# The low part of every second weight chunk of the second feed-forward stage: from a VectorE subtraction to a negated ScalarE copy and an adding transfer

## The chip, the cores and the metric

The kernel runs on one core of one Trainium2 chip. The metric is the device time of one execution in microseconds. The core has five engines with instruction streams of their own: TensorE (PE) multiplies matrices, VectorE (DVE), ScalarE (ACT) and GpSimd (POOL) work on elements, and SyncE (SP) issues transfers. Transfers run on 16 DMA engines. ScalarE and GpSimd can issue transfers too. In the profile's lines PEld is TensorE's load of its stationary operand.

## The reference

One block of a network on 256 tokens of width 2048, in float32: a gated feed-forward stage (inner width 5632), a mixer of two branches (a state-space scan and a gated spatial unit) whose results are merged, a second gated feed-forward stage, and a last norm.

```python
def swiglu_ffn(h, w_gate, w_up, w_down):
    return (jax.nn.silu(h @ w_gate) * (h @ w_up)) @ w_down
...
        h = rms_norm(x, ffn1_norm[i])
        x = x + 0.5 * swiglu_ffn(h, ffn1_w_gate[i], ffn1_w_up[i], ffn1_w_down[i])
        h = rms_norm(x, mix_norm[i])
        proj = h @ w_in[i]
...
        merged = g_a * (y_a @ w_branch_a[i]) + g_b * (y_b @ w_branch_b[i])
        x = x + merged @ w_out[i]
        h = rms_norm(x, ffn2_norm[i])
        x = x + 0.5 * swiglu_ffn(h, ffn2_w_gate[i], ffn2_w_up[i], ffn2_w_down[i])
    return rms_norm(x, final_norm)
```

The change lies in the line before the last: the weights of the second `swiglu_ffn`.

## The kernel before

All weights are read once, as chunks of 128 x 2048 float32 (1 MB), in one list `chunks` of 356 that is filled by `add` and `add_ffn` (lines 104 to 134) in the order in which they are used. Chunks 0 to 131 are the first feed-forward stage, 132 to 223 the mixer and its output, 224 to 355 the second feed-forward stage. A feed-forward stage has three groups (4, 4 and 3 blocks of 512 inner columns). In a group each block takes four gate chunks and four up chunks, and then the group's down weights follow (16, 16 and 12 chunks).

TensorE multiplies in the type float32r, which keeps fewer bits than float32. To keep the accuracy, each operand is held as two float32r parts: the high part is the value rounded to float32r, and the low part is the rest, value minus high part. A product is then the sum of three: high by high, high by low, and low by high. For a weight chunk `split_to` (line 151) does this: ScalarE copies the raw chunk into `whi` (line 148, which rounds it), and VectorE subtracts `whi` from the raw chunk into `wlo` (line 149).

A chunk has four columns of work for TensorE (`step`, line 212, called by `job`): each takes 512 columns of the chunk and issues six matmuls, for two halves of the tokens the lines 216 (`whi`), 217 (`wlo`) and 218 (`whi`). So a chunk is 24 matmuls of 512 columns.

The order of work is written out by hand (a manual schedule). `take` calls `tick` before each column of work. At the first column of chunk c, `tick` first issues what was left to do for earlier results (hooks that fall due, then the evacuations in `pend`) and then `split_to(c + 2)` (LOOK = 2). That issues the load of chunk c + 4 on SP's queue (`load_to`, line 139) and the split of chunk c + 2. There are three raw buffers, three `whi` and three `wlo` (NRAW and NSPL). So chunk c + 2 takes the `whi` and `wlo` of chunk c - 1, and its split can begin when TensorE has ended that chunk; the load of chunk c + 4 takes the raw buffer of chunk c + 1 and can begin when that one has been split. Each engine works through its instructions in the order in which they were issued.

The evacuations of the feed-forward stages are: after a gate job two Silu passes on ScalarE (line 318), after an up job a multiplication on VectorE (line 328) and, two columns of work later, transposes on TensorE (line 258) with a split of the result on ScalarE and VectorE (lines 244 and 245); after a down job an addition on VectorE (line 293). The start of the last group's down part (`down_out`, line 1014) issues a 1 MB load on POOL's queue, of the final norm's gain into the tile `fin` (line 1017). It is POOL's only work in the second feed-forward stage.

Of the kernel before, what the change touches and what calls it, by code (L numbers as in the profile page):

```python
# [12 lines left out]
AF = mybir.ActivationFunctionType  # L13
ALU = mybir.AluOpType
# [12 lines left out]
SUB = 2048  # L27
# [18 lines left out]
def f(ap):  # L46
    return ap.bitcast(F32)
# [3 lines left out]
def kernel(  # L51
# [31 lines left out]
    act, dve, pe, pool = nc.scalar, nc.vector, nc.tensor, nc.gpsimd  # L83
# [20 lines left out]
    chunks = []  # L104

    def add(w, a=0, n=None):
        chunks.extend(w[i] for i in range(a, w.shape[0] if n is None else a + n))

    def add_ffn(wg, wu, wd, first):
        j, d = 0, 0  # L110
        for n in GROUPS:
            for _ in range(n):
                if j == 0 and first is not None:
                    add(first)
                else:
                    i = j - (first is not None)
                    add(wg, 4 * i, 4)
                    add(wu, 4 * i, 4)
                j += 1
            add(wd, d, 4 * n)  # L120
            d += 4 * n
# [8 lines left out]
    add(w_ga, 12, 4)  # L130
    add(w_ba)
    add(w_out)
    add_ffn(w2g, w2u, w2d, None)
    NSUB = len(chunks)

# [3 lines left out]
    def load_to(i):  # L139
        while st["load"] <= min(i, NSUB - 1):  # L140
            j = st["load"]
            t = wp.tile([P, SUB], F32, tag="raw", name="raw", bufs=NRAW)
            nc.sync.dma_start(out=t, in_=chunks[j])
            raws[j] = t
            st["load"] += 1

    def split_piece(hi, lo, r, s):
        act.activation(out=hi[:, s], in_=r[:, s], func=AF.Copy)  # L148
        dve.tensor_tensor(out=lo[:, s], in0=r[:, s], in1=f(hi[:, s]), op=ALU.subtract)  # L149

    def split_to(i):
        while st["split"] <= min(i, NSUB - 1):
            j = st["split"]
            load_to(j + NRAW - 1)
            r = raws.pop(j)
            hi = wp.tile([P, SUB], F32R, tag="whi", name="whi", bufs=NSPL)
            lo = wp.tile([P, SUB], F32R, tag="wlo", name="wlo", bufs=NSPL)
            split_piece(hi, lo, r, slice(0, SUB))
            splits[j] = (hi, lo)
            st["split"] += 1  # L160

# [12 lines left out]
    def tick():  # L174
        for fn in hooks.pop(st["tick"], ()):
            fn()
        while pend:
            pend.pop(0)()
        if st["off"] == 0:
            split_to(st["sub"] + LOOK)  # L180
            splits.pop(st["sub"] - 1, None)
        credit[0] += credit[1]
        while fillers and credit[0] >= 1.0:
            try:
                next(fillers[0])
                credit[0] -= 1.0
            except StopIteration:
                fillers.pop(0)
        if not fillers:
            credit[0] = 0.0  # L190
        st["tick"] += 1
# [572 lines left out]
    st["split"] = 1  # L764
    split_h1(2)
    split_to(1)
    split_h1(4)
    for i in range(5):
# [379 lines left out]
```

## Time and profile before

| what | us |
|---|---|
| median of 2 runs (2087.6 and 2088.61) | 2088.11 |
| the profiled execution, as timed | 2085.11 |
| the profiled execution's span, first to last instruction | 2083.3 |
| line 149 on VectorE, the low part, 355 whole chunks: each | 2.292 |
| line 148 on ScalarE, the high part, 355 whole chunks: each | 1.915 |
| lines 216 to 218 on TensorE, one matmul as shown | 0.39 |

The span is what the profile's positions and shares refer to; the time as timed is 1.8 us longer. Matmuls are pipelined: one is shown as lasting 0.39 us, but a new one starts about every 0.23 us. A line of the timeline gives start, duration, engine, line of the kernel, operation, output and inputs, and in brackets how long the engine was idle before it and whom it waited for. A line of the waits gives the waiting engine and line, whom it waited for, and the total in us, how often, and the longest. A line of the stages gives the busy time and number of instructions of TensorE, its weight load, VectorE, ScalarE and POOL, then the granted TensorE clock (1.00 is full), the share of time in which the DMA engines were busy, and GB/s. A line of the transfers gives how many, the size of each, and the median time from issue to landing.

### The profile page before, as it was taken

To read this page: it belongs to the slowest core of one execution; us is meant where nothing else is said; L and a number is where in the kernel's file an instruction comes from. 1 tells how busy PE (TensorE), PEld (TensorE's weight loads), DVE (VectorE), ACT (ScalarE), POOL (GpSimd) and SP (SyncE) were. 2 spreads that over 40 slices of the span, in tenths; PEclk is the share of its full clock that TensorE was granted. 3 is DMA by queue.
4 is the path that set the end of the run, shared out by engine and by line. 5 is a ranking of instruction groups with operands and counts; after the bars stand their busy time and mean duration, and the time that the engine had idled before them with its cause. 6 is when DMAs were issued, how large, how long until landed. Compare 5 with 4: busy or idle time off the path is not lost. (4 is left out here: it accounts for less than half of the span.)

```text
span 2083.3 us, 23136 instructions
## 1 busy us (share of the span) xinstructions
PE 2034.3 (98%) x9764; PEld 1681.5 (81%) x9764; DVE 1126.6 (54%) x1095; ACT 862.8 (41%) x702; POOL 73.0 (4%) x135
## 2 busy tenths in 40 slices
PE   8999999999999999999989899999999999999997
PEld 6888888887888888878777788888888888888886
DVE  4765665546664555556555665554454444544454
ACT  5543344443334454443333544443433334333443
POOL 0000001111000000011100000000000000000000
PEclk9999999999999999999999999999999999999999
DMA  7457766555655455566555455555555555555553
GB/s 305 182 197 240 244 222 210 190 201 180 221 204 195 171 191 213 191 236 211 200 200 188 170 182 182 202 198 186 191 193 191 193 184 187 194 199 185 189 180 117
DMA packets 65769, 412.20 MB, mean 198 GB/s; under 512 B 10192, under 2 KB 10592, under 8 KB 19840
## 3 DMA queue, kind: packets, MB, share of 16 engines
q1 hardware_dynamic: 52848, 376.49, 50.6%
q0 software_dynamic: 10800, 30.03, 4.5%
q10 hardware_dynamic: 2016, 4.20, 0.6%
q8 instruction: 76, 1.25, 0.2%
q14 instruction: 29, 0.24, 0.0%
HBM read 398.21 MB, written 12.45 MB: 197 GB/s over the span
## 5 line engine op out<-in xcount | busy, mean ns | idle before, releaser
L149 DVE TENSOR_TENSOR wlo<-raw,whi 128x2048 fp32r<-128x2048 f32 (+1 forms) x359 | 815.8, 2274 | 789.3 <-ACT whi L148 789.2
L148 ACT ACTIVATE whi<-raw 128x2048 fp32r<-128x2048 f32 (+1 forms) x359 | 681.5, 1901 | 907.1 <-PE acc L218 832.0
L216 PE MATMUL acc<-whi,h 128*128 128x512 f32 x1856 | 728.7, 393 | 5.9 <-ACT whi L148 5.9
L217 PE MATMUL acc<-wlo,h 128*128 128x512 f32 x1856 | 724.8, 391 | 4.8 <-DVE wlo L149 4.8
L218 PE MATMUL acc<-whi,h 128*128 128x512 f32 x1856 | 724.2, 390 | 0.0
L216 PEld LDWEIGHTS acc<-whi,h 128*128 128x128 f32 x1856 | 349.7, 188 | 79.5 <-ACT whi L148 7.0
L217 PEld LDWEIGHTS acc<-wlo,h 128*128 128x128 f32 x1856 | 349.7, 188 | 78.0 <-DVE wlo L149 6.7
L218 PEld LDWEIGHTS acc<-whi,h 128*128 128x128 f32 x1856 | 349.6, 188 | 73.2
L216 PE MATMUL acc<-whi,gt 128*128 128x512 f32 x704 | 276.0, 392 | 0.0
L218 PE MATMUL acc<-whi,gt 128*128 128x512 f32 x704 | 276.0, 392 | 0.0
L217 PE MATMUL acc<-wlo,gt 128*128 128x512 f32 x704 | 275.1, 391 | 0.0
L217 PEld LDWEIGHTS acc<-wlo,gt 128*128 128x128 f32 x704 | 132.5, 188 | 28.7
L218 PEld LDWEIGHTS acc<-whi,gt 128*128 128x128 f32 x704 | 132.6, 188 | 28.0
L216 PEld LDWEIGHTS acc<-whi,gt 128*128 128x128 f32 x704 | 132.6, 188 | 27.9
L318 ACT ACTIVATE t<-acc,rc 128x512 f32<-128x512 f32 x44 | 27.9, 686 | 69.4 <-PE acc L218 69.4
L216 PE MATMUL acc<-whi,mT 128*128 128x512 f32 x128 | 50.2, 392 | 0.0
L218 PE MATMUL acc<-whi,mT 128*128 128x512 f32 x128 | 49.8, 389 | 0.0
L217 PE MATMUL acc<-wlo,mT 128*128 128x512 f32 x128 | 49.8, 389 | 0.0
L293 DVE SCALAR_TENSOR_TENSOR x_sb<-acc,x_sb 128x1024 f32<-128x1024 f32 x27 | 33.1, 1225 | 27.6 <-PE acc L218 27.6
L273 ACT ACTIVATE junk<-x_sb 128x512 bf16<-128x512 f32 x32 | 20.2, 631 | 64.6 <-DVE x_sb L293 53.0
L328 DVE SCALAR_TENSOR_TENSOR t<-acc,rc,t 128x512 f32<-128x512 f32 x44 | 31.0, 746 | 21.7 <-PE acc L218 21.6
L244 ACT ACTIVATE gt<-q 128x512 fp32r<-128x512 f32 x44 | 23.9, 596 | 31.3 <-PE q L258 31.3
(195 smaller groups left out, 1031.2 us busy)
## 6 DMA issues: line engine op xcount, KB each, us to landing
raw<-in_w1d_dram SPq DMA_DIRECT2D x44, 1024.0 KB, 4.9
raw<-in_w2g_dram SPq DMA_DIRECT2D x44, 1024.0 KB, 4.8
raw<-in_w2u_dram SPq DMA_DIRECT2D x44, 1024.0 KB, 4.8
raw<-in_w2d_dram SPq DMA_DIRECT2D x44, 1024.0 KB, 4.8
raw<-in_w1g_dram SPq DMA_DIRECT2D x40, 1024.0 KB, 4.9
raw<-in_w1u_dram SPq DMA_DIRECT2D x40, 1024.0 KB, 4.9
raw<-in_w_in_dram SPq DMA_DIRECT2D x24, 1024.0 KB, 4.8
raw<-in_w_gb_dram SPq DMA_DIRECT2D x16, 1024.0 KB, 4.9
```

What stands on the lines that cost most here:

```text
L148: act.activation(out=hi[:, s], in_=r[:, s], func=AF.Copy)
L149: dve.tensor_tensor(out=lo[:, s], in0=r[:, s], in1=f(hi[:, s]), op=ALU.subtract)
L216: pe.matmul(acc[:, h, :], lhsT=lhs[:, k, 0, t], rhs=hi, start=first, stop=False)
L217: pe.matmul(acc[:, h, :], lhsT=lhs[:, k, 0, t], rhs=lo, start=False, stop=False)
L218: pe.matmul(acc[:, h, :], lhsT=lhs[:, k, 1, t], rhs=hi, start=False, stop=last)
L244: act.activation(out=dst[:, :, 0, :], in_=src, func=AF.Copy)
L273: act.activation(out=j, in_=x_sb[:, h, m * N:m * N + N], func=AF.Square, accum_out=ssq[:, h, m:m + 1])
L293: dve.scalar_tensor_tensor(out=xs, in0=acc, scalar=scale, in1=xs, op0=ALU.mult, op1=ALU.add)
L318: act.activation(out=s[:, h, :], in_=acc[:, h, :], func=AF.Silu, scale=rc(h))
L328: dve.scalar_tensor_tensor(out=s[:, h, :], in0=acc[:, h, :], scalar=rc(h), in1=s[:, h, :], op0=ALU.mult, op1=ALU.mult)
```

## The change

`SECOND` is set to the number of chunks before the second feed-forward stage plus 8, which is 232. From there on the chunks with an even number take another way to their low part. ScalarE makes the high part as before. It then makes a second copy of the raw chunk with the factor -1 into `wlo`, which is the negated high part. A transfer issued by GpSimd then reads the same chunk from HBM a second time and adds it to what `wlo` holds. VectorE does nothing for these chunks. The load of the raw chunk on SP's queue, the odd chunks, and all chunks before 232 are as they were.

```diff
     add(w_out)
+    SECOND = len(chunks) + 8
     add_ffn(w2g, w2u, w2d, None)
     NSUB = len(chunks)
...
             lo = wp.tile([P, SUB], F32R, tag="wlo", name="wlo", bufs=NSPL)
-            split_piece(hi, lo, r, slice(0, SUB))
+            if j >= SECOND and j % 2 == 0:
+                act.activation(out=hi, in_=r, func=AF.Copy)
+                act.activation(out=lo, in_=r, func=AF.Copy, scale=-1.0)
+                pool.dma_start(out=lo, in_=chunks[j], accum_op=ALU.add)
+            else:
+                split_piece(hi, lo, r, slice(0, SUB))
             splits[j] = (hi, lo)
             st["split"] += 1
```

## The prediction

> **What bounds the kernel now.** I read first the head of the page (busy time by engine), then the waits, then the timeline of one chunk in the second feed-forward stage, and last the transfers and the granted clock.
>
> ```profile
> span 2083.3 us, 23136 instructions
> PE 2034.3 (98%) x9764; PEld 1681.5 (81%) x9764; DVE 1126.6 (54%) x1095; ACT 862.8 (41%) x702; POOL 73.0 (4%) x135
> PE acc L217 <- DVE wlo L149: 4.8, 4, 1.8
> DVE wlo L149 <- ACT whi L148: 346.2, 131, 4.3
> ACT whi L148 <- PE acc L218: 365.4, 114, 3.6
> 1800.00:2060.00 260.00, 260.00 (x1161) 215.51 (x1160) 126.42 (x72) 101.34 (x73) 0.00 (x0) 1.00 0.51 182
> ```
>
> TensorE is busy for 2034.3 of 2083.3 us. The third line is its longest total of waits for a low part, 4.8 us in the whole run. The next two lines are the waits from 1330 to 2060 us alone, the second feed-forward stage: ScalarE waits for TensorE to free a weight buffer (114 times), VectorE waits for ScalarE; TensorE has no wait at all in that view. The last line is the stage 1800 to 2060 us: TensorE 260.00 of 260.00 us, VectorE 126.42, POOL 0, clock 1.00, the DMA engines 0.51 busy. So this stage is TensorE alone, and VectorE time taken out of it is worth nothing. It can only lose.
>
> How much a low part may be late is read from one chunk:
>
> ```profile
> 1398.26 1.92 ACT L148 ACTIVATE whi<-raw 128x2048 fp32r<-128x2048 f32 x1 [3.52 <-PE acc L218]
> 1403.70 1.92 ACT L148 ACTIVATE whi<-raw 128x2048 fp32r<-128x2048 f32 x1 [3.52 <-PE acc L218]
> 1405.65 2.29 DVE L149 TENSOR_TENSOR wlo<-raw,whi 128x2048 fp32r<-128x2048 f32 x1 [3.15 <-ACT whi L148]
> 1403.50 0.39 PE L216 MATMUL acc<-whi,h 128*128 128x512 f32 x1
> 1403.73 0.39 PE L217 MATMUL acc<-wlo,h 128*128 128x512 f32 x1
> ```
>
> A chunk takes 1403.70 - 1398.26 = 5.44 us. When TensorE has ended chunk c-1, its buffers go to chunk c+2: the ScalarE copy starts at 1403.70, as chunk c starts on TensorE (1403.50; its first low-part matmul is at 1403.73). Chunk c+2's first low-part matmul comes two chunks on, at 1403.73 + 10.88 = 1414.61, so the low part has 10.91 us from the start of the copy. VectorE is done at 1405.65 + 2.29 = 1407.94: 6.7 us to spare.
>
> **The change, part by part.** The chunks are 0 to 355; the second stage begins at 224, so the condition takes the even ones from 232 to 354: 62 chunks, one in each pair of 10.88 us.
>
> *Removed:* 62 subtractions of 2.29 us, 142 us of VectorE. Worth 0: TensorE waits for none of them, and 142 us of VectorE would hide nothing else.
>
> *Second ScalarE pass:* the same shape as the copy, 1.92 us, x62 = 119 us. ScalarE has 101.34 of 260 us busy, so there is room; but the pass stands in the path of the low part, which is there at 1.92 + 1.92 + 0.06 = 3.9 us (0.06 for two hand-overs; from 1403.70 + 1.92 to 1405.65 one took 0.03). It frees the raw buffer then, against 4.24 us before, so SP's loads start no later. Queued behind it on ScalarE are the copies of the next chunk (3.5 us idle before them) and the evacuations in mid-chunk, at most 1.92 us later with their results due chunks later: 0. A gate evacuation in front of the copy takes about 1.2 us off the room of one chunk in eight; that falls into the stall below or the slack beside it: 0, at most 10 x 1.2 = 12 us.
>
> *The adding transfer:* it is issued by POOL once the negated part is there, and may take 10.91 - 3.9 = 7.0 us from issue to landing. Call that time D. No transfer of before adds into its destination; the nearest rows are:
>
> ```profile
> raw<-in_w2g_dram SPq DMA_DIRECT2D x44, 1024.0 KB, 4.8
> x_sb<-in_xk_dram POOLq DMA_DIRECT2D x1, 2048.0 KB, 11.1
> fin<-in_gf_dram POOLq DMA_DIRECT2D x1, 1024.0 KB, 7.5
> ws_sb<-in_wst_dram POOLq DMA_DIRECT2D x1, 512.0 KB, 5.4
> 1342.28 0.60 POOL L1017 DMA_DIRECT2D fin<-in_gf_dram  x1 [198.82 <-PE acc L218]
> ```
>
> A megabyte lands in 4.8 us from SP's queue and in 7.5 us from POOL's, beside the same raw loads. Adding reads two megabytes (weights and the destination) and writes one. Per half megabyte POOL's rows grow by 7.5 - 5.4 = 2.1 us, so a second megabyte read makes 7.5 + 4.2 = 11.7; the row that moves two megabytes says 11.1. Low end: 4.8 (it lands like a raw load; nothing can be gained below, since nobody waits). High end: 2 x 7.5 = 15 (reading the destination and adding do not overlap at all). I take 11.1, the row nearest in bytes read: it is issued by POOL and shares the engines with other loads.
>
> The Trainium skill, page "DMA: Bandwidth & Descriptors", section "Anatomy of one DMA", gives such a POOL transfer 2.0 us plus bytes/436e3: 4.4 us for one megabyte, an estimate of 6.8 us for two. By that rule D is under 7.0 and the change costs nothing; the traced 7.5 and 11.1 stand against it, and the sum goes by the rows.
>
> *From D to time.* A transfer later than 7.0 us makes TensorE wait x = D - 7.0 = 4.1 us. The wait is not paid at every pair. The copy for chunk e+2 starts when chunk e-1 ends, before the wait of e, so e's wait is slack for e+2: the next even chunk is on time, and only the one after waits again. That is 31 waits: 31 x 4.1 = 127 us.
>
> *The clock after a wait.* The trace has such waits in the mixer:
>
> ```profile
> 1061.00 0.39 PE L216 MATMUL acc<-whi,h 128*128 128x512 f32 x1
> 1062.62 0.50 PE L217 MATMUL acc<-wlo,h 128*128 128x512 f32 x1 [1.24 <-DVE wlo L149]
> 1062.96 0.40 PE L218 MATMUL acc<-whi,h 128*128 128x512 f32 x1
> 1063.20 0.39 PE L216 MATMUL acc<-whi,h 128*128 128x512 f32 x1
> ...
> 1107.84 0.50 PE L216 MATMUL acc<-whi,h 128*128 128x512 f32 x1 [0.22 <-ACT whi L148]
> 1110.17 0.64 PE L217 MATMUL acc<-wlo,h 128*128 128x512 f32 x1 [1.82 <-DVE wlo L149]
> 1110.60 0.63 PE L218 MATMUL acc<-whi,h 128*128 128x512 f32 x1
> 1113.59 0.49 PE L216 MATMUL acc<-whi,h 128*128 128x512 f32 x1
> 1113.92 0.39 PE L217 MATMUL acc<-wlo,h 128*128 128x512 f32 x1
> 1114.15 0.40 PE L218 MATMUL acc<-whi,h 128*128 128x512 f32 x1
> ...
> 1110.00:1115.00 5.00, 4.83 (x14) 3.86 (x15) 5.00 (x5) 1.39 (x1) 0.00 (x0) 0.66 0.58 210
> ```
>
> After a wait of 1.24 us the matmuls follow each other by 0.24 us as ever. After one of 1.82 us they follow by 0.43 us, from 1110.17 to 1113.59, and the stage's granted clock is 0.66. Eight steps of 0.43 in place of 0.23 are 1.6 us, with the next (0.33) 1.7 us. A wait of 4.1 us is well past that, so each costs 1.7 us more: 31 x 1.7 = 53 us. (It also lends slack to the next even chunk, which needs none.) The Trainium skill, page "TensorE: Matmul & The Clock Gate", section "Part 1: The HAM clock gate", says that about 3.4 us of idleness halves the clock and about 3.4 us of work restores it; the 3.42 us of slow matmuls agree, while here 1.82 us of waiting were enough. By that rule alone waits of 2 to 3 us would cost no clock; at 4.1 us both give the same sum.
>
> *DMA engines.* One raw load occupies them for 0.51 x 5.44 = 2.77 us. Four chunks need 4 x 2.77 and two adding transfers 2 x 5.54 (two megabytes each): 22.2 us, in a stretch of 21.76 + 4.1 + 1.7 = 27.6 us. They are not the bound, but 0.8 busy. Raw loads have 3 x 5.44 - 4.2 = 12.1 us before they are needed, against 4.8: hidden; without that cover each late microsecond would stop TensorE.
>
> *POOL's queue.* One other issue lies in this stage, the final gain (fin), at 1342.28 before. It is now behind the adding transfers ahead of it in the program, with the third group's down part (chunk 344, which is (344 - 224) x 5.44 = 653 us into the stage), so it leaves some 640 us later. Its first reader starts there after three chunks (16.3 us) and it lands in 7.5: hidden, though one adding transfer shares with it, at most 2.8 us once.
>
> **Sum.** 127 + 53 = 180 us on the profiled execution's span of 2083.3 (2085.11 as timed): 2263 as a span. The runs' median is 2088.11, 3.0 above that execution's time: 2088 + 180 = 2268 us.
>
> **The rivals.** Below, 2% is 42 us, about what a measurement of this kernel can tell from no change.
>
> *Covered, no slower.* The second read is pipelined with the first and the transfer lands like a raw load, D from 4.8 to 7.0: 2088 us. With the 7.5 of fin, x is 0.5 and the cost 31 x 0.5 = 16 us: 2104. It decides up to x = 1.24, D = 8.2, below which no clock is lost: 38 us, 2126. For it: 4.8 us for raw loads, engines half idle. Against: every POOL row of a megabyte or more is above 7.0 before any addition.
>
> *The transfer is itself the bound.* If adding runs at a quarter of the copy's rate, it holds the engines 4 x 2.77 = 11.1 us; four chunks then need 11.1 + 22.2 = 33.3 us, 11.5 above 21.76, x31 = 357 us: 2445. With D = 15, not bound but strung out, x = 8.0: 31 x 9.7 = 301, so 2389. For it: no row shows the adding rate, and small POOL transfers are slow in this trace. Against: rows here show bytes, not operations, as the cost.
>
> *Waits without the clock.* If the waits leave the clock at 1.00, as after 1.24 us, the 53 us go: 2215.
>
> That the change doesn't do what it says has a narrow form: the second read is not taken and D is fin's 7.5; that is the first rival.
>
> The Trainium skill, page "Collectives: The Full Stack", section "The bandwidth ceiling", puts a reduction in the DMA engines at half the rate of a copy because of two reads, and the addition itself at nothing; no run here shows it. By it the second rival falls away.
>
> **How the numbers follow.** D between 9 and 13, with the clock lost (the last-named rival in it): 0.56; its own range is 2203 to 2327, from 31 x 3.7 and 31 x 7.7. Covered or nearly: 0.16, of which 0.01 is faster by over 2%, for which no row shows a wait to remove. The transfer as bound or strung out: 0.28. Slower by over 2% is 0.56 + 0.28 = 0.84, within it 0.15. The range goes from 2115, which leaves out most of the covered case (0.12), to 2445, the bound at a quarter of the rate (0.08 beyond).
>
> **What would show it.** The adding issues' median to landing: about 11 us; 7 or under is the first rival, 15 or over the second. TensorE's waits for wlo: some 31 of about 4 us, on every second even chunk (waits on all 62 say that my slack argument is wrong). Granted clock in 1800 to 2060: about 0.95 or lower, 1.00 if the waits are harmless. DMA share: about 0.8; near 1 is the second rival. VectorE lower by about 142 us and ScalarE up by 119. The forecast fails if D is under 8.2, or if raw loads come late and ScalarE is seen waiting for them.

## The result and the profile after

The changed kernel takes 2289.38 us in the median of 2 runs (2289.0 to 2289.76), against 2088.11 before: 1.097 times as long, with an interval of 1.094 to 1.100. That is 201 us more. The forecast was 2268, so 180 of these 201 us, and slower with a chance of 0.84. The profiled execution's span grew from 2083.3 to 2287.2 us, by 204 us.

First the head of the page after (busy time by engine), then two stages inside the second feed-forward stage (columns as before: busy time of TensorE, weight load, VectorE, ScalarE, POOL, then clock, DMA share, GB/s).

```profile
span 2287.2 us, 23313 instructions
PE 2102.8 (92%) x9764; PEld 1722.3 (75%) x9764; DVE 985.4 (43%) x1033; ACT 974.1 (43%) x764; POOL 126.2 (6%) x197
```

```profile
1380.00:2000.00 620.00, 523.43 (x2116) 422.01 (x2115) 128.74 (x82) 257.82 (x159) 37.06 (x43) 0.91 0.81 220
2000.00:2264.00 264.00, 223.75 (x922) 181.17 (x921) 58.14 (x40) 114.46 (x81) 16.02 (x19) 0.92 0.78 213
```

TensorE has the same 9764 matmuls, but its busy time rose from 2034.3 to 2102.8 us, by 68.5. The granted clock in the stage fell from 1.00 to 0.91, and TensorE now stands idle in it. VectorE lost 141 us and ScalarE gained 111: the work did move, to no use.

The list of TensorE's waits in this stage was empty before. These are its only entries now (total, times, longest), and below them the adding transfers in the list of issues (number, size, median from issue to landing):

```profile
PE acc L223 <- DMA wlo<-in_w2d_dram: 49.6, 11, 6.2
PE acc L223 <- DMA wlo<-in_w2u_dram: 45.3, 10, 6.1
PE acc L223 <- DMA wlo<-in_w2g_dram: 41.9, 10, 5.3
```

```profile
wlo<-in_w2d_dram POOLq DMA_DIRECT2D x22, 1024.0 KB, 11.5
wlo<-in_w2g_dram POOLq DMA_DIRECT2D x20, 1024.0 KB, 11.5
wlo<-in_w2u_dram POOLq DMA_DIRECT2D x20, 1024.0 KB, 11.1
```

There are 11 + 10 + 10 = 31 waits for 62 transfers, 136.8 us in all, 4.4 us each. These 136.8 us and the 68.5 us of longer busy time are 205.3 us, against 203.9 us by which the span grew: the two account for all of it. One of the 31 in the timeline of TensorE, with the issue of its transfer on POOL and of the raw load on SP ahead of it (the lines are put together from the three engines):

```profile
1807.79 0.33 SPq L144 DMA_DIRECT2D raw<-in_w2u_dram  x1
1808.05 0.87 POOL L162 DMA_DIRECT2D wlo<-in_w2u_dram  x1 [16.90 <-ACT wlo L161]
1814.72 0.39 PE L222 MATMUL acc<-whi,h 128*128 128x512 f32 x1
1819.24 0.79 PE L223 MATMUL acc<-wlo,h 128*128 128x512 f32 x1 [4.13 <-DMA wlo<-in_w2u_dram]
1819.83 0.63 PE L224 MATMUL acc<-whi,h 128*128 128x512 f32 x1
1820.26 0.63 PE L222 MATMUL acc<-whi,h 128*128 128x512 f32 x1
...
1825.38 0.42 PE L222 MATMUL acc<-whi,h 128*128 128x512 f32 x1
1825.64 0.40 PE L223 MATMUL acc<-wlo,h 128*128 128x512 f32 x1
1825.88 0.40 PE L224 MATMUL acc<-whi,h 128*128 128x512 f32 x1
```

The transfer leaves at 1808.05, 0.26 us after a raw load, and the matmul that needs it starts 11.2 us later. After the wait the matmuls follow each other by 0.43 us until 1825.38, and by 0.23 to 0.26 us from there on.

### The profile page after: what moved, and what is told of

Same layout as the page of the kernel before. It is cut to its first block, busy times and chain, and to the rows that moved or that the text cites. A ratio compares the mean times of both kernels' runs of the same rounds, so it can differ in the third digit from the quotient of the medians.

```text
span 2287.2 us, 23313 instructions
## 1 busy us (share of the span) xinstructions
PE 2102.8 (92%) x9764; PEld 1722.3 (75%) x9764; DVE 985.4 (43%) x1033; ACT 974.1 (43%) x764; POOL 126.2 (6%) x197
## 4 chain that ended last, share of the span: by engine, by line
PE 28%; DMA 16%; issue 6%; DVE 1%; ACT 1%; POOLq 0%; POOL 0%; ACTq 0%; DVEq 0%
PE acc L223 9%; PE acc L224 9%; PE acc L222 8%; DMA wlo<-in_w2d_dram 5%; DMA wlo<-in_w2u_dram 5%; DMA wlo<-in_w2g_dram 5%; PE q L264 1%; DVE wlo L150 0%; PE acc L240 0%; PE acc L238 0%; PE acc L239 0%; DMA tab<-stash_w 0%; ACT whi L149 0%; DMA yT<-y_dr 0%; DMA y_dr<-y 0%
## 5 line engine op out<-in xcount | busy, mean ns | idle before, releaser
L150 DVE TENSOR_TENSOR wlo<-raw,whi 128x2048 fp32r<-128x2048 f32 (+1 forms) x297 | 673.6, 2270 | 1026.4 <-ACT whi L149 1026.3
L149 ACT ACTIVATE whi<-raw 128x2048 fp32r<-128x2048 f32 (+1 forms) x297 | 562.6, 1897 | 773.0 <-PE acc L224 485.1
L223 PE MATMUL acc<-wlo,h 128*128 128x512 f32 x1856 | 743.5, 401 | 91.6 <-DMA wlo<-in_w2u_dram 45.3
L222 PE MATMUL acc<-whi,h 128*128 128x512 f32 x1856 | 742.2, 400 | 4.9 <-ACT whi L149 4.9
L224 PE MATMUL acc<-whi,h 128*128 128x512 f32 x1856 | 738.9, 398 | 0.0
L222 PEld LDWEIGHTS acc<-whi,h 128*128 128x128 f32 x1856 | 357.8, 193 | 82.8 <-ACT whi L149 6.0
L224 PEld LDWEIGHTS acc<-whi,h 128*128 128x128 f32 x1856 | 359.0, 193 | 75.4
L223 PE MATMUL acc<-wlo,gt 128*128 128x512 f32 x704 | 285.6, 406 | 49.6 <-DMA wlo<-in_w2d_dram 49.6
L222 PE MATMUL acc<-whi,gt 128*128 128x512 f32 x704 | 283.2, 402 | 0.0
L224 PE MATMUL acc<-whi,gt 128*128 128x512 f32 x704 | 282.8, 402 | 0.0
L223 PEld LDWEIGHTS acc<-wlo,gt 128*128 128x128 f32 x704 | 137.5, 195 | 83.7 <-DMA wlo<-in_w2d_dram 54.2
L160 ACT ACTIVATE whi<-raw 128x2048 fp32r<-128x2048 f32 x62 | 118.6, 1913 | 173.9 <-PE acc L224 173.9
L222 PEld LDWEIGHTS acc<-whi,gt 128*128 128x128 f32 x704 | 136.8, 194 | 30.6
L161 ACT ACTIVATE wlo<-raw 128x2048 fp32r<-128x2048 f32 x62 | 117.6, 1897 | 0.0
L251 DVE TENSOR_TENSOR gt<-q,gt 128x512 fp32r<-128x512 f32 x44 | 28.3, 684 | 93.4 <-ACT gt L250 93.4
L299 DVE SCALAR_TENSOR_TENSOR x_sb<-acc,x_sb 128x1024 f32<-128x1024 f32 x27 | 33.1, 1224 | 45.7 <-PE acc L224 45.7
```

The source lines that it names most:

```text
L160: act.activation(out=hi, in_=r, func=AF.Copy)
L161: act.activation(out=lo, in_=r, func=AF.Copy, scale=-1.0)
L222: pe.matmul(acc[:, h, :], lhsT=lhs[:, k, 0, t], rhs=hi, start=first, stop=False)
L223: pe.matmul(acc[:, h, :], lhsT=lhs[:, k, 0, t], rhs=lo, start=False, stop=False)
L224: pe.matmul(acc[:, h, :], lhsT=lhs[:, k, 1, t], rhs=hi, start=False, stop=last)
L251: dve.tensor_tensor(out=dst[:, :, 1, :], in0=src, in1=f(dst[:, :, 0, :]), op=ALU.subtract)
```

## The experiments

Two explanations were to be told apart. By the first (latency), each adding transfer lands too late for its chunk, the wait lends slack to the next even chunk, and the clock drops after each wait. By the second (rate), the DMA engines have too much to move and set the pace. All edits below are made to the changed kernel, and ratios are to the kernel before, whose median in the runs beside them was 2084.9 to 2085.4 us; sums below take 2085.

### Half the transfers

```diff
-            if j >= SECOND and j % 2 == 0:
+            if j >= SECOND and j % 4 == 0:
```

> Only chunks 232, 236 and so on (31 in place of 62) take the new way. Theory: the wait of one even chunk is slack for the next, so the 62 gave only 31 waits, and 31 adding chunks still give 31 waits of about 4.4 us with the clock lost after each: 2260 to 2290 us, nearly the time of all 62. Rival, each adding transfer has its price: half of the 201 us is gone, 2188 us.

Measured: 2290.09 us, ratio 1.098 (1.097 to 1.100). Half of the adding transfers were taken away and nothing was gained. TensorE's waits for them:

```profile
PE acc L223 <- DMA wlo<-in_w2d_dram: 48.9, 11, 6.3
PE acc L223 <- DMA wlo<-in_w2u_dram: 46.2, 10, 7.6
PE acc L223 <- DMA wlo<-in_w2g_dram: 42.4, 10, 5.2
```

Again 31 waits and 137.5 us. In the change, then, every other adding transfer was free, because the wait before it gave it the time that it lacked. The DMA share here is 0.61 from 1380 to 2000 us, against 0.81, and the time is the same, so a rate is not what decided. The transfers land in 11.1 to 11.2 us, hardly sooner than with all 62: the total load of the DMA engines did not make them late either.

### The transfer without the addition, and no transfer

```diff
-                pool.dma_start(out=lo, in_=chunks[j], accum_op=ALU.add)
+                pool.dma_start(out=lo, in_=chunks[j])
```

> The same transfer without the addition, so the low part holds the whole weight. Theory: it lands in about 7.5 us instead of 11.3, waits of 0.5 us, too short to lose the clock: about 2105 us. Rival, any POOL transfer here takes 11 us because of the company of the raw loads: about 2289 us.

Measured: 2122.75 us, ratio 1.017 (1.015 to 1.019). The plain transfers landed in 7.1 us in the median (5.1 to 9.3). TensorE waited 18 times, 20.7 us in all, where 31 waits of 7.1 + 3.9 - 10.9 = 0.1 us would make 3: the transfers vary, a late one costs, and an early one pays nothing back. Its busy time rose by 2054.2 - 2034.3 = 19.9 us; in its timeline four waits are followed by slow matmuls, which make about 6.6 of these, and most of the rest are single steps from matmul to matmul of 0.3 to 0.5 us, many of them right after a wait. The rival is out: company alone does not make 11 us.

With the last line of the edit left out altogether:

> The negated copy stays, the adding transfer is left out, so the low part holds the negated high part. Theory: the second ScalarE pass is hidden, 2088 us and no wait of TensorE. Rival, ScalarE's queue is what delays TensorE: above 2110 us.

Measured: 2085.34 us, ratio 1.000 (0.999 to 1.001), and no wait of TensorE in the stage. The second ScalarE pass and the subtraction that is no longer made are both worth nothing.

### Issued earlier, or due later

The next two shorten the lateness without touching the transfer. One makes the negated part first:

```diff
-                act.activation(out=hi, in_=r, func=AF.Copy)
                 act.activation(out=lo, in_=r, func=AF.Copy, scale=-1.0)
+                act.activation(out=hi, in_=r, func=AF.Copy)
                 pool.dma_start(out=lo, in_=chunks[j], accum_op=ALU.add)
```

> ScalarE makes the negated part first and the high part after it, so the transfer can leave about 1.85 us earlier. Theory (latency): 31 waits of about 2.5 us, the clock still lost: 31 x (2.5 + 1.9) = 138, about 2226 us. Rival, the DMA engines' rate sets the pace: no change, 2289 us.

Measured: 2145.70 us, ratio 1.029 (1.027 to 1.031): the loss falls from 201 to 61 us, more than expected. The transfers also landed sooner, 10.1 us in the median, so that by the forecast's rule the waits should come to 31 x (2.05 + 10.1 - 10.9) = 39 us; the list of waits has 42.0 us, but in 36. At a mean of 1.2 us most of them no longer cost any clock: the busy time rose by 25.4 us instead of 68.5. Six stretches of slow matmuls are left, about 11 us of these; most of the rest are single steps of 0.3 to 0.5 us, as in the run with plain transfers.

The other makes the low part due later, by holding back its eight matmuls to the end of the chunk (`wait` is true in the adding chunks, `late` is a list of what is held back):

```diff
             pe.matmul(acc[:, h, :], lhsT=lhs[:, k, 0, t], rhs=hi, start=first, stop=False)
-            pe.matmul(acc[:, h, :], lhsT=lhs[:, k, 0, t], rhs=lo, start=False, stop=False)
-            pe.matmul(acc[:, h, :], lhsT=lhs[:, k, 1, t], rhs=hi, start=False, stop=last)
+            if wait:
+                late.append((acc[:, h, :], lhs[:, k, 0, t], lo, last))
+            else:
+                pe.matmul(acc[:, h, :], lhsT=lhs[:, k, 0, t], rhs=lo, start=False, stop=False)
+            pe.matmul(acc[:, h, :], lhsT=lhs[:, k, 1, t], rhs=hi, start=False, stop=last and not wait)
+        if wait and st["off"] == 0:
+            for a, w, lo, end in late:
+                pe.matmul(a, lhsT=w, rhs=lo, start=False, stop=end)
+            late.clear()
```

> In the adding chunks the 16 matmuls of the high part run first and the 8 of the low part last, so the low part is due 15 x 0.23 = 3.4 us later; nothing else changes. Theory: waits of about 1.0 us, too short to lose the clock: 2088 + 31 = about 2120 us. If the clock is lost after 1 us too: about 2180. If the DMA engines are the bound: 2289.

Measured: 2173.07 us, ratio 1.040 (1.037 to 1.044). The expectation missed: 88 us are lost, not 31. The transfers took longer here, 12.1 us in the median with 7.9 to 14.9 between the ends, as the raw loads beside them did (8.0 us for the up weights, against 6.2 in the change). With 12.1 the rule gives 31 x (3.9 + 12.1 - 10.9 - 3.4) = 53 us of waits, and the list has 58.2; some are up to 4.0 us long, and the busy time rose by 31.8 us. The total of the waits agrees with the rule once D is right, but not their number: there are 45, of 1.3 us in the mean. A short wait no longer lends the next transfer all that it lacks. Why D went to 10.1 us in the one run and to 12.1 us in the other was not separated.

Both together (the transfer now also stands ahead of the high part in the program):

> Negated part and transfer first (1.85 us earlier) and low parts last (3.4 us later). Latency alone: the transfer is covered, 2088 us. But four chunks need 4 x 2.94 + 2 x 5.16 = 22.1 us of the DMA engines (from their shares after the change) against 21.76 us of TensorE: they now come up to the bound, so 2095 to 2130 us.

Measured: 2089.13 us, ratio 1.002 (1.001 to 1.003). Two waits are left, 1.4 us in all. Its stage from 1380 to 2000 us:

```profile
1380.00:2000.00 620.00, 619.44 (x2772) 513.07 (x2771) 165.16 (x104) 335.89 (x209) 48.84 (x57) 1.00 0.97 284
```

TensorE is busy for 619.44 of 620.00 us at full clock, beside DMA engines that are 0.97 busy. The expected loss by rate did not come: here a share near 1 made hardly any wait, as the transfers had time to spare. All 62 adding transfers are made, so all but some 4 us of the loss were lateness. The change becomes harmless in this way, but no more than that: VectorE's time was not what the kernel lacked. A longer lead by a fourth pair of split buffers stays unmeasured: even with two raw buffers in place of three it does not fit, since a pool of 33.1 KB per partition finds only 25.7 KB left in the core's memory.

### The clock by itself

As in the first experiment, with 16 matmuls into a scratch bank ahead of the first low-part matmul, where TensorE would stand idle (`fill` is true at the first column of an adding chunk):

```diff
+            if fill and h == 0:
+                q = ms.tile([P, N], F32, tag="ms", name="q")
+                for i in range(16):
+                    pe.matmul(q, lhsT=lhs[:, k, 0, t], rhs=hi, start=True, stop=True)
```

> As e1, with 16 matmuls of 512 columns into a scratch bank (3.6 us of work that is thrown away) ahead of the first low-part matmul of each adding chunk, where TensorE waits anyway. Theory: the waits stay, TensorE is busy in most of them and keeps its clock, so the time falls by 31 x 2.2 = 68 us below e1, to about 2220 us. Rival, the slow matmuls after a wait have another cause than the idle time: e1's time or more.

Measured: 2233.81 us, ratio 1.071 (1.069 to 1.074), 56 us less than with 31 idle waits, and somewhat less than the 68 expected. One of the waits in its timeline (line 229 is the scratch work):

```profile
1814.29 3.79 PE L229 MATMUL q<-whi,h 128*128 128x512 f32 x16
1818.54 0.50 PE L230 MATMUL acc<-wlo,h 128*128 128x512 f32 x1 [0.47 <-DMA wlo<-in_w2g_dram]
1818.88 0.39 PE L231 MATMUL acc<-whi,h 128*128 128x512 f32 x1
1819.11 0.40 PE L225 MATMUL acc<-whi,h 128*128 128x512 f32 x1
```

The low part comes as late as ever (1818.54 is 4.25 us after 1814.29), but after it the matmuls follow each other by 0.23 us almost at once, and the granted clock from 1380 to 2000 us is 1.00, against 0.92 without the scratch work. Work that is thrown away, in a wait that must be waited anyway, saved 56 us: 1.8 us for each wait.

### Where the rate does decide

For every chunk instead of every second, first with both of the moves above, then as the change has it:

```diff
-            if j >= SECOND and j % 2 == 0:
+            if j >= SECOND:
```

> As e6, but for every chunk from 232 on (124, even and odd). The latency is covered as in e6. The DMA engines need 2.94 + 5.17 = 8.1 us for a chunk against 5.44 us of TensorE, so here they are the bound: 124 x 2.7 = 330, about 2420 us at a DMA share near 1. If even this is hidden: 2089 us.

> As the change, but for every chunk from 232 on. By latency alone three chunks would take 5.44 + 15.2 us, 6.9 us each; by the DMA engines' rate 8.1 us each. Theory: the rate is now the longer one, so the same 2420 us as with both moves, perhaps up to 2480 with the clock. If latency decides: 2088 + 124 x 1.5 = 2270 and the clock's loss above it.

Measured: 2318.28 us, ratio 1.111 (1.109 to 1.113), with both moves, and 2390.27 us, ratio 1.146 (1.142 to 1.149), without. The stages from 1380 to 2000 us, with both moves and without:

```profile
1380.00:2000.00 620.00, 492.44 (x2082) 380.89 (x2081) 28.95 (x38) 327.74 (x199) 72.40 (x84) 0.99 1.03 282
```

```profile
1380.00:2000.00 620.00, 496.25 (x1962) 384.20 (x1961) 27.71 (x37) 309.94 (x188) 69.02 (x80) 0.93 1.01 268
```

With both moves the DMA engines are now the bound: they move 282 GB/s, no more than the 284 with the same moves at every second chunk, and the adding transfers land in 17.8 us in the median instead of 9.9. (Their share is 1.03, more than there is, so the page must count some time twice.) A chunk takes 5.44 + (2318 - 2085) / 124 = 7.3 us, not the expected 8.1, so the sum of the engines' busy times overstates what they need by about a tenth. Without the moves the span is 78 us longer, and 57 us of that are TensorE's busy time (2137.2 against 2079.9 us): at a clock of 0.93 the waits are longer and cost it, at 0.99 they are many and short. The expectation that both would take the same time missed.

### The load beside the transfer

Here `load_to` is also given the queue on which the load goes out:

```diff
-            load_to(j + NRAW - 1)
+            adding = j >= SECOND and j % 2 == 0
+            if not adding:
+                load_to(j + NRAW - 1)
...
                 pool.dma_start(out=lo, in_=chunks[j], accum_op=ALU.add)
+                load_to(j + NRAW - 1, pool)
```

> As the change, but the raw load that becomes due at an adding chunk goes out on POOL's queue right behind the adding transfer, not on SP's queue beside it. The bytes are the same. Theory: part of the 11.3 us to landing is the company of that load (plain transfers took 7.1, adding occupies the engines 2.6 us longer): without it about 9.5 us, waits of about 2.5 us, 31 x (2.5 + 1.7) = 130, near 2215 us. Rival, an adding transfer takes 11 us by itself: near 2289 us.

Measured: 2462.02 us, ratio 1.180 (1.178 to 1.182). Both sides of the expectation missed. ScalarE's longest waits, and from the list of issues the transfers on POOL's queue:

```profile
ACT whi L162 <- DMA raw<-in_w2d_dram: 218.1, 22, 11.0
ACT whi L162 <- DMA raw<-in_w2g_dram: 197.5, 19, 11.7
ACT whi L162 <- DMA raw<-in_w2u_dram: 159.6, 20, 10.8
```

```profile
raw<-in_w2d_dram POOLq DMA_DIRECT2D x22, 1024.0 KB, 12.5
wlo<-in_w2d_dram POOLq DMA_DIRECT2D x22, 1024.0 KB, 10.5
```

A raw load behind an adding transfer on POOL's queue lands 12.5 us after its issue. It is issued some 3.9 + 0.6 us after the copy of one even chunk has begun, and the copy of the next even chunk needs it: 3.9 + 0.6 + 12.5 = 17.0 us from copy to copy, in place of 10.88. The time agrees: 2462 - 2085 = 377 us over 62 pairs are 6.1, and 10.88 + 6.1 = 17.0. So the late raw load took over as the cause. The transfer itself came down only to 10.5 us in this run, and the question of how much the company costs stays half open. The nearest answer is at the end of the traces, when SP has no load left to issue: the last adding transfer of the change lands in 8.1 us, against a median of 11.3, and the last plain one of the run above in 5.2, against 7.1. By these two single transfers some 3 of the 11.3 us would be company, and the addition would cost about 3 us by itself.

## Why the prediction was right

**That it would only lose, and by latency.** Right. Leaving out the transfer gives 2085 us, halving the number of transfers changes nothing, and moving their issue and due time gives 2089 with all 62 made.

**D, 11.1 us.** The median was 11.3 (8.1 to 13.2). The row of two megabytes, taken for the bytes read, stood near it, and that it stood so near is partly luck. That transfer ran in the kernel's first microseconds, beside DMA engines that were 0.96 to 1.00 busy (5 to 15 us); POOL's rows of half a megabyte before lie anywhere from 5.1 to 10.5 us; and the median of the same adding transfer moved from 9.9 to 12.1 us when only the order around it changed. What the doubling rests on is better shown: the plain transfer took 7.1 us. In DMA-engine time a plain one held the engines (0.120 x 2120.6 - 0.045 x 2083.3) / 62 = 2.59 us and an adding one (0.181 x 2287.2 - 0.045 x 2083.3) / 62 = 5.17 us, from the shares of POOL's queue on the pages: twice as much. The Trainium skill, page "Collectives: The Full Stack", section "The bandwidth ceiling", has a reduction at half the rate of a copy because of its two reads; the factor of two agrees, while no run here shows that the second read is the reason. The Trainium skill, page "DMA: Bandwidth & Descriptors", section "Anatomy of one DMA", gives 4.4 us for one megabyte, and for two an estimate of 6.8 us; the runs show 7.1 and 11.3 beside raw loads, and 5.2 and 8.1 for the last ones without.

**31 waits, not 62.** Right, and the surest part for this change: 31 waits were counted, some 29 us apart (one in four chunks), and half of the transfers cost as much as all. The count holds only while a wait is as long as the next transfer is late: at a mean wait of 1.2 or 1.3 us there were 36 and 45. Each was 4.4 us instead of 4.1, so the term is 137 us against 127.

**The clock, 1.7 us for each wait.** The mechanism was right and this term was mis-sized: the busy time rose by 68.5 us, 2.2 us for each of 31, against 53. The step that failed is the price read from a single row. In that row the matmuls were slow for 3.42 us. In the trace after, the slow stretch lasted about 3 to 6 us. Its end follows a grid. In three of the waits it came with these matmuls:

```profile
1480.63 0.43 PE L224 MATMUL acc<-whi,h 128*128 128x512 f32 x1
...
1538.66 0.42 PE L222 MATMUL acc<-whi,h 128*128 128x512 f32 x1
...
1825.38 0.42 PE L222 MATMUL acc<-whi,h 128*128 128x512 f32 x1
```

The distances, 58.03 and 286.72 us, are 17.00 and 84.00 times 3.413 us. The granted clock in the periods of this grid around the wait shown earlier (columns as in the stages):

```profile
1815.18:1818.60 3.42, 0.00 (x0) 0.00 (x0) 0.00 (x0) 3.42 (x4) 0.00 (x0) 1.00 0.97 252
1818.60:1822.01 3.41, 2.77 (x7) 2.19 (x8) 0.00 (x0) 1.18 (x1) 0.85 (x1) 0.50 0.84 274
1822.01:1825.43 3.42, 3.42 (x10) 2.65 (x9) 0.00 (x0) 0.00 (x0) 0.00 (x0) 0.50 1.01 292
1825.43:1828.84 3.41, 3.41 (x16) 2.80 (x15) 0.00 (x0) 1.10 (x1) 0.00 (x0) 1.00 1.03 214
```

The clock changes only at a tick. It falls to 0.50 after the period in which TensorE stood idle; the wait goes on 0.64 us past that tick, into a period that then stays at 0.50 as a whole (the last section counts when), so it pays for nearly two. Of the 31 waits 18 lost one such period and 13 lost two. The row from before had met the short case, and the sum had one period for each. The Trainium skill, page "TensorE: Matmul & The Clock Gate", section "Part 1: The HAM clock gate", gives a free-running window of 3413 ns, and the grid agrees.

**DMA engines at 0.8.** Right: 0.81 and 0.78, and not the bound. The rival that they would be is false for every second chunk; for every chunk, with both moves, they were.

**Covers.** VectorE's 141 us and ScalarE's pass were worth nothing, as forecast. The gain (fin) was issued at 2182.89 behind an adding transfer and took 15.5 us to land instead of 7.5; TensorE has no wait for it.

## What to carry to other kernels

A step that is moved to a transfer is judged by its latency against the lead of its buffers: here 3.9 + 11.3 us against 10.9. Total lateness then goes by how many waits there can be, not by how many transfers are late, since a wait in a pipeline with lead lends time to what is already under way; so taking half of them away may gain nothing. Where TensorE must wait for about 2 us or more, count the slow matmuls after it as well (here 2.2 us for each wait of 4.4), and look first for matmuls that do not need the late operand.

## What the runs showed of the hardware

No fixed length of a wait loses the clock. Three of the waits where the negated part was made first:

```profile
1618.32 0.50 PE L223 MATMUL acc<-wlo,gt 128*128 128x512 f32 x1 [2.20 <-DMA wlo<-in_w2d_dram]
...
1801.66 0.50 PE L223 MATMUL acc<-wlo,h 128*128 128x512 f32 x1 [1.84 <-DMA wlo<-in_w2u_dram]
1802.00 0.39 PE L224 MATMUL acc<-whi,h 128*128 128x512 f32 x1
1802.23 0.40 PE L222 MATMUL acc<-whi,h 128*128 128x512 f32 x1
...
2087.13 0.50 PE L223 MATMUL acc<-wlo,gt 128*128 128x512 f32 x1 [1.86 <-DMA wlo<-in_w2d_dram]
2087.47 0.40 PE L224 MATMUL acc<-whi,gt 128*128 128x512 f32 x1
2087.93 0.60 PE L223 MATMUL acc<-wlo,gt 128*128 128x512 f32 x1
2088.33 0.63 PE L224 MATMUL acc<-whi,gt 128*128 128x512 f32 x1
...
2091.32 0.42 PE L222 MATMUL acc<-whi,gt 128*128 128x512 f32 x1
```

After 1.84 us the matmuls go on by 0.23 us, and so they do after 2.20 us; after 1.86 us they go on for 0.8 us and then slow down to 0.43, from 2087.93 to 2091.32: one period of 3.4 us. So the clock is taken away at a tick as well. Counted back from there in periods of 3.413 us, ticks lie at 1616.9 and 1801.2, inside the waits of 2.20 and 1.84 us, which leaves at most 1.4 us of idle time in one period; the 1.86 us lie in one period whole.

Counted so in the second feed-forward stage of all traces here, the idle time of TensorE within one period decides. No period with less than 1.8 us idle cost the clock, every one with more than 1.95 us did, and between these the runs differ. Once at half, the clock came back after every period with at most 0.59 us idle and after none with 0.61 us or more (237 periods). These are counts from the traces; no run was made to test them.

An adding transfer held the DMA engines twice as long as a plain one (5.17 against 2.59 us). DMA engines 0.97 busy made TensorE wait only twice, 1.4 us in all.
